# Product banks of PSUM in tiles of two, and rotary tables fetched one part earlier

## The chip, the cores and the metric

The kernel runs on one core of one Trainium2 chip, in one launch. The metric is the device time of one execution in microseconds (us). Three runs of the kernel before took 2540.79, 2544.62 and 2546.06 us; the median is 2544.62 us.

The engines are named as in the profile: PE (TensorE) multiplies matrices, PEld is its weight load, DVE is VectorE, ACT is ScalarE, POOL is GpSimd, and SP only issues transfers here. PE writes its products into PSUM, of which the program uses eight banks of 128 x 512 fp32. Another engine has to read a product out of its bank (evacuate it) before that bank can take a new one.

## The reference, cut to what matters

The first block is a hybrid mixer (projections, dilated window attention, a chunked state-space scan) and a feed-forward part. The second block has two layers on two streams of 256 positions, x and ctx, each 1024 wide:

```
for l in range(2):
    x  = x  + 0.5 * mx[2] * swiglu_2(modulate(rms_norm(x),  mx[0], mx[1]), *ffn1)
    xc = xc + 0.5 * mc[2] * swiglu_2(modulate(rms_norm(xc), mc[0], mc[1]), *ffn1)
    h, hc = modulate(rms_norm(x), ...), modulate(rms_norm(xc), ...)
    y, y_c = mix_window_diff(h, hc, ..., rope_head)          # layer 0
    y, _   = mix_mla_neighbourhood(h, hc, ..., rope_mla)     # layer 1
    x = x + mx[5] * y
    x = x + 0.5 * mx[8] * swiglu_2(modulate(rms_norm(x), mx[6], mx[7]), *ffn2)
    (layer 0 does the last two for xc, too)

def swiglu_2(h, w_gate, w_up, w_down):
    return (jax.nn.silu(h @ w_gate) * (h @ w_up)) @ w_down
```

`mx` and `mc` are nine vectors each, products of the condition with `w_mod`. `rope_head` and `rope_mla` are tables of cosines and sines that turn queries and keys. Layer 0 mixes by a windowed attention with sinks and a differential one (each head has two score maps); layer 1 by a latent attention (queries of six latent blocks, `cq`) and a neighbourhood attention with a bias looked up in `d_rpb`. All is fp32.

## The kernel before, in words

Every weight is loaded as fp32 and split in two: ACT casts it to a reduced form (`wh`, L114), DVE subtracts that from it (`wl`, L115). Activations are split likewise (`ah` and `al`, or `hh` and `hl`). A product of 128 output rows is a unit: for each of eight blocks of the contraction three matmuls, `wh*ah`, `wh*al`, `wl*ah` (L133 to L135), 24 in all, into one bank. With both streams side by side a matmul is 512 columns wide, with one stream 256.

A feed-forward part (`ffn`) runs a gate unit and an up unit for each of 22 blocks of the hidden width, and 24 down units between and after them. The gate's product is evacuated by ACT (silu, L409), the up product by DVE (`g<-g,pm`, L413), then ACT casts `hh` (L119) and DVE subtracts `hl` (L120). Down units are evacuated by DVE into the residual (L443).

The products stand in a pool `ps` of four tiles of one bank, tile name `pm` (L79, `psum`, L163). Two other pools of two banks each hold small sums (`pt`, `pa`). Weights go through five buffers for the raw load (`wraw`) and five for the two parts; short-lived tiles share ten buffers (`t1`).

Between the units stand background pieces (`weave`): each loads 512 KB of `w_mod` into a `wraw` buffer, and DVE multiplies it with the condition, once for each stream (`junk`, L981). There are 144 of them.

The order of the instructions on each engine is fixed when the program is built: a list scheduler with its own cost model and priorities puts them in order, and pools hand out buffers in that order. On the chip each engine works through its own list, and waits on semaphores for the others. Nothing is reordered there.

The mixers (`mix_ab` of layer 0, `mix_cd` of layer 1) load their tables `cos` and `sin` at their start by two transfers that ACT issues (L1181, L1182; L1397, L1398). DVE multiplies them with gains into tables for queries and keys (L1093, L1094). In layer 1 DVE's list has these ahead of the x stream's normalized input (`y`, L351, which ACT shifts to `ah`, L355). At the same place POOL issues a write of 1778 KB to DRAM, `rpb` (L1404), from which biases of the neighbourhood attention are read later. The attention parts take a bank for the scores of each head (L1257, L1317, L1580, L1602): DVE finds the row maximum (L1265, L1321, L1549) and ACT takes the exponential (L1100).

Of the kernel before, what the change touches and what calls it, by code (L numbers as in the profile page):

```python
# [16 lines left out]
T = 256  # L17
# [51 lines left out]
class Builder:  # L69
    def __init__(self, ctx, tc, A):  # L70
# [8 lines left out]
        self.ps = ctx.enter_context(tc.tile_pool(name="ps", bufs=4, space=PSUM))  # L79
# [82 lines left out]

    def psum(self):  # L163
        return self.ps.tile([128, 512], F32, name="pm")
# [996 lines left out]
def mix_ab(K, streams):  # L1161
# [86 lines left out]
    def attend_a(s, t, half):  # L1248
# [5 lines left out]
        def scores():  # L1254
            for b in range(2):
                for kv in range(2):
                    rows = slice(64 * kv, 64 * kv + 64)  # L1257
                    p = K.psum()
                    nc.tensor.matmul(p[:, :nk], qa[s][rows, 2 * half + b, t * 128:(t + 1) * 128], ka[rows, k0:k0 + nk],  # L1259
                                     start=True, stop=True)  # L1260
                    if s == "x":
                        o = p[:, (1 - t) * 128:(2 - t) * 128]
                        nc.vector.tensor_tensor(o, o, amask[:, t], op=ALU.add)
                    m = mneg[:, kv, b:b + 1]
                    nc.vector.tensor_reduce(out=m, in_=p[:, :nk], axis=AX.X, op=ALU.max, negate=True)  # L1265
                    h = 4 * kv + 2 * half + b
                    nc.vector.tensor_tensor(m, m, nsink[:, h:h + 1], op=ALU.min)
                    pr[kv][b] = softmax_tail(K, sp, p, nk, m, den[:, kv, b:b + 1])
# [40 lines left out]
    def attend_b(s, t, hd):  # L1309
# [81 lines left out]
def mix_cd(K, streams):  # L1391
# [4 lines left out]
    cos, sin = K.t1("cos"), K.t1("sin")  # L1396
    nc.scalar.dma_start(cos[r96], A["mla_cos"])  # L1397
# [492 lines left out]
```

## Time and profile before

| what | us |
|---|---|
| median of three runs | 2544.62 |
| the profiled execution | 2545.32 |
| its span in the trace | 2543.5 |
| PE busy | 2457.1 (97%) |
| DVE busy | 1642.2 (65%) |
| ACT busy | 1070.2 (42%) |

The span is the time from the first to the last instruction of the profiled execution. An engine's busy time is a sum over the whole span; how near an engine is to being the bound differs from stage to stage. The stages, by their start in the trace: mixer of block 1 from 0, its feed-forward part from 460, layer 0 with feed-forward 1 from 670, `mix_ab` from 1040, its output from 1300, feed-forward 2 from 1330; layer 1 with feed-forward 1 from 1700, `mix_cd` from 2060, attention from 2243, output and feed-forward 2 from 2350.

### The profile page before, as it was taken

The page shows a single profiled execution, that of the slowest core. Times are in us where ns is not written, and L with a number is a line of the kernel's source. Part 1 is how long each engine was busy: PE and PEld are TensorE (multiplying, and loading weights), DVE is VectorE, ACT ScalarE, POOL GpSimd, SP SyncE. Part 2 cuts the span into 40 slices and gives each one's busy share as a digit, 9 for nine tenths or more (in the row PEclk, how much of TensorE's full clock was granted, in tenths as well). Part 3 has the DMA queues.
Part 4 walks back from the last instruction along what each step waited for, and adds up shares of the span by engine and source line. Part 5 has one row for each costly group of instructions (what it writes and reads, how often), then busy time and mean ns, then how long its engine had stood idle before and what let it go on. Part 6 is the DMA issues. An engine that isn't in the chain of part 4 may idle for free.

```text
span 2543.5 us, 38370 instructions
## 1 busy us (share of the span) xinstructions
PE 2457.1 (97%) x15104; PEld 2122.3 (83%) x15104; DVE 1642.2 (65%) x3009; ACT 1070.2 (42%) x1934; POOL 15.4 (1%) x20
## 2 busy tenths in 40 slices
PE   6999999999999999999999999999999968999999
PEld 6999999999988888885598888888888857866999
DVE  4667777787867564767767666566545344667554
ACT  4657565535522222436743222243222234555443
POOL 0000000000000000000000000000000000000000
PEclk9999899999999999999999999999999988999999
DMA  8555455676455553431025545325555342232563
GB/s 227 148 156 161 144 163 182 210 246 203 162 166 167 164 168 99 130 98 51 1 75 178 170 150 170 128 91 178 171 166 164 103 96 74 98 95 82 172 185 125
DMA packets 117204, 363.66 MB, mean 143 GB/s; under 512 B 21050, under 2 KB 28730, under 8 KB 117024
## 3 DMA queue, kind: packets, MB, share of 16 engines
q1 hardware_dynamic: 114512, 355.73, 44.2%
q0 software_dynamic: 1008, 3.09, 1.0%
q10 hardware_dynamic: 1504, 2.40, 0.3%
q8 instruction: 119, 1.95, 0.3%
q14 instruction: 61, 0.50, 0.1%
HBM read 357.34 MB, written 3.82 MB: 142 GB/s over the span
## 4 chain that ended last, share of the span: by engine, by line
PE 70%; DVE 2%; DMA 2%; ACT 1%; issue 0%; ACTq 0%
PE pm L133 20%; PE pm L134 20%; PE pm L135 20%; PE pt L1120 1%; DMA sin<-mla_sin 1%; PE pa L1027 1%; PE pt L1051 1%; PE pa L1574 1%; PE pm L1319 1%; PE pm L1582 1%; PE pm L1259 0%; PE pa L1335 0%; PE pa L1296 0%; PE pm L1604 0%; PE pm L1145 0%; PE pa L1147 0%
## 5 line engine op out<-in xcount | busy, mean ns | idle before, releaser
L133 PE MATMUL pm<-ah,wh 128*128 128x256 f32 (+2 forms) x3096 | 1012.7, 329 | 46.4 <-ACT ah L355 35.6
L134 PE MATMUL pm<-al,wh 128*128 128x256 f32 (+2 forms) x3096 | 1007.1, 326 | 1.2 <-DVE al L356 1.1
L135 PE MATMUL pm<-ah,wl 128*128 128x256 f32 (+2 forms) x3096 | 1005.2, 325 | 0.0
L114 ACT CAST wh<-wraw 128x1024 fp32r<-128x1024 f32 (+4 forms) x535 | 540.3, 1013 | 1057.1 <-PE pm L134 850.0
L115 DVE TENSOR_TENSOR wl<-wraw,wh 128x1024 fp32r<-128x1024 f32 (+4 forms) x535 | 627.2, 1175 | 242.2 <-ACT wh L114 240.0
L133 PEld LDWEIGHTS pm<-ah,wh 128*128 128x128 f32 (+1 forms) x3096 | 588.6, 191 | 107.2 <-ACT ah L355 37.3
L134 PEld LDWEIGHTS pm<-al,wh 128*128 128x128 f32 (+1 forms) x3096 | 590.7, 191 | 54.2 <-issue 2.4
L135 PEld LDWEIGHTS pm<-ah,wl 128*128 128x128 f32 (+1 forms) x3096 | 590.6, 191 | 51.4 <-issue 1.7
L134 PE MATMUL pm<-hl,wh 128*128 128x512 f32 (+1 forms) x934 | 317.1, 339 | 0.0
L133 PE MATMUL pm<-hh,wh 128*128 128x512 f32 (+1 forms) x934 | 316.6, 339 | 0.0
L135 PE MATMUL pm<-hh,wl 128*128 128x512 f32 (+1 forms) x934 | 316.4, 339 | 0.0
L981 DVE SCALAR_TENSOR_TENSOR junk<-wraw,cactc 128x1024 f32<-128x1024 f32 x112 | 137.2, 1225 | 213.2 <-DMA wraw<-w_mod 212.8
L981 DVE SCALAR_TENSOR_TENSOR junk<-wraw,cactx 128x1024 f32<-128x1024 f32 x144 | 176.0, 1222 | 41.0 <-DMA wraw<-w_mod 38.6
L133 PEld LDWEIGHTS pm<-hh,wh 128*128 128x128 f32 x934 | 175.9, 188 | 21.2 <-issue 0.2
L135 PEld LDWEIGHTS pm<-hh,wl 128*128 128x128 f32 x934 | 175.9, 188 | 20.9
L134 PEld LDWEIGHTS pm<-hl,wh 128*128 128x128 f32 x934 | 175.9, 188 | 20.9
L119 ACT CAST hh<-g 128x512 fp32r<-128x512 f32 (+1 forms) x113 | 59.2, 526 | 162.1 <-DVE g L413 162.1
L413 DVE TENSOR_TENSOR g<-g,pm 128x512 f32<-128x512 f32 (+1 forms) x113 | 64.0, 566 | 58.7 <-PE pm L135 57.3
L120 DVE TENSOR_TENSOR hl<-g,hh 128x512 fp32r<-128x512 f32 (+1 forms) x113 | 63.8, 566 | 0.3
L409 ACT ACTIVATE g<-pm 128x512 f32<-128x512 f32 (+1 forms) x116 | 56.1, 489 | 2.5 <-PE pm L135 2.3
L443 DVE SCALAR_TENSOR_TENSOR xc<-pm,mcol0c,xc 128x256 f32<-128x256 f32 x56 | 26.9, 480 | 46.0 <-PE pm L135 45.8
L307 DVE TENSOR_TENSOR acc<-acc,sq 128x256 f32<-128x256 f32 x105 | 42.3, 419 | 13.7 <-ACT sq L306 13.4
(421 smaller groups left out, 2228.7 us busy)
## 6 DMA issues: line engine op xcount, KB each, us to landing
wraw<-w_mod SPq DMA_DIRECT2D x144, 512.0 KB, 4.1
wraw<-f1g SPq DMA_DIRECT2D x44, 512.0 KB, 3.7
wraw<-f1u SPq DMA_DIRECT2D x44, 512.0 KB, 4.2
wraw<-f2g SPq DMA_DIRECT2D x44, 512.0 KB, 3.7
wraw<-f2u SPq DMA_DIRECT2D x44, 512.0 KB, 4.0
wraw<-f1d SPq DMA_DIRECT2D x32, 512.0 KB, 4.0
wraw<-f2d SPq DMA_DIRECT2D x32, 512.0 KB, 3.7
wraw<-w_xbc SPq DMA_DIRECT2D x24, 512.0 KB, 3.6
```

What stands on the lines that cost most here:

```text
L114: nc.scalar.copy(h[:, :f], raw[:, :f])
L115: nc.vector.tensor_tensor(lo[:, :f], raw[:, :f], h[:, :f].bitcast(F32), op=ALU.subtract)
L119: self.nc.scalar.copy(h, src)
L120: self.nc.vector.tensor_tensor(lo, src, h.bitcast(F32), op=ALU.subtract)
L133: nc.tensor.matmul(out, h[:, c], ah, start=first, stop=False)
L134: nc.tensor.matmul(out, h[:, c], al, start=False, stop=False)
L135: nc.tensor.matmul(out, lo[:, c], ah, start=False, stop=last)
L307: nc.vector.tensor_tensor(self.acc[key], self.acc[key], sq, op=ALU.add)
L409: nc.scalar.activation(half(g["g"], s), p, AF.Silu)
L413: nc.vector.tensor_tensor(t, t, p, op=ALU.mult)
L443: self.nc.vector.scalar_tensor_tensor(x, p, gate, x, op0=ALU.mult, op1=ALU.add)
L981: nc.vector.scalar_tensor_tensor(junk, raw, 1.0, K.cact[s], op0=ALU.mult, op1=ALU.mult, accum_out=K.mcol[layer, s][:, j:j + 1])
```

## The change

The pool `ps` has two tiles of two banks instead of four of one. `psum()` hands out the first half of a tile, and at the next call its second half. `psum2()` hands out a whole tile, and the attention parts take one for the scores of two heads (or of two score maps); DVE then finds both row maxima in one instruction, adds masks and biases in one, and ACT takes two exponentials as before. The neighbourhood attention loads its biases for two heads at once. The tables `cos` and `sin` are fetched by a piece at the end of the preceding feed-forward part's list, by POOL's queue, into two of the ten `t1` buffers, where they stay until the mixer has used them.

```diff
@@ class Builder
-        self.ps = ctx.enter_context(tc.tile_pool(name="ps", bufs=4, space=PSUM))
+        self.ps = ctx.enter_context(tc.tile_pool(name="ps", bufs=2, space=PSUM))
+        self.half = None
...
+    def psum2(self):
+
+        self.half = None
+        return self.ps.tile([128, 2, 512], F32, name="pm")
+
     def psum(self):
-        return self.ps.tile([128, 512], F32, name="pm")
+
+        if self.half is None:
+            t = self.psum2()
+            self.half = t[:, 1]
+            return t[:, 0]
+        t, self.half = self.half, None
+        return t
@@ mix_ab (mix_cd likewise, with mla_cos, mla_sin)
-    cos, sin = K.t1("cos"), K.t1("sin")
-    nc.scalar.dma_start(cos, A["rope_cos"])
-    nc.scalar.dma_start(sin, A["rope_sin"])
+    cos, sin = K.rope
@@ differential attention
         def scores():
+            p = K.psum2()
             for m in range(2):
                 rows = slice(64 * m, 64 * m + 64)
-                p = K.psum()
-                nc.tensor.matmul(p[:, :nk], qb[s][rows, hd, t * 128:(t + 1) * 128], kb[rows, hd, k0:k0 + nk],
+                nc.tensor.matmul(p[:, m, :nk], qb[s][rows, hd, t * 128:(t + 1) * 128], kb[rows, hd, k0:k0 + nk],
                                  start=True, stop=True)
-                nc.vector.tensor_reduce(out=mneg[:, m:m + 1], in_=p[:, :nk], axis=AX.X, op=ALU.max, negate=True)
-                es.append(softmax_tail(K, sp, p, nk, mneg[:, m:m + 1], den[:, m:m + 1]))
+            nc.vector.tensor_reduce(out=mneg, in_=p[:, :, :nk], axis=AX.X, op=ALU.max, negate=True)
+            for m in range(2):
+                es.append(softmax_tail(K, sp, p[:, m], nk, mneg[:, m:m + 1], den[:, m:m + 1]))
...
@@ block2
+        def rope(layer=layer):
+
+            K.rope = K.t1("cos"), K.t1("sin")
+            rows = slice(0, 96 if layer else 128)
+            for t, n in zip(K.rope, ("cos", "sin")):
+                nc.gpsimd.dma_start(t[rows], A[("mla_" if layer else "rope_") + n])
+
         K.ffn(A[f"f1g{layer}"], A[f"f1u{layer}"], [A[f"f1d{layer}{i}"] for i in range(3)], both,
-              lambda s, m: K.mod(layer, s, 2)(m), hid_p, K.pieces(40), norms(3))
+              lambda s, m: K.mod(layer, s, 2)(m), hid_p, K.pieces(40) + [rope], norms(3))
```

The order of the instructions changes with it. Three places follow; the line numbers of the changed kernel are a little higher (L133 to L135 become L134 to L136, L413 becomes L425, L981 L993, L1093 L1105, L1441 L1450).

The first place is layer 0, feed-forward 2, at the end of an up unit of the 17th to 22nd hidden blocks. On PE, before, one unit follows another, each with a tile of its own (`pm_15885` is the up unit):

```order
L133 MATMUL pm_15885<-ah_5605,wh_15806 128x512
L134 MATMUL pm_15885<-al_5606,wh_15806 128x512
L135 MATMUL pm_15885<-ah_5605,wl_15807 128x512
L133 MATMUL pm_15927<-ah_5605,wh_15848 128x512
L134 MATMUL pm_15927<-al_5606,wh_15848 128x512
L135 MATMUL pm_15927<-ah_5605,wl_15849 128x512
```

Now the same up unit has the first half of `pm_15617` (weights `wh_15539`), the gate unit after it has the second half (`wh_15581`):

```order
L134 MATMUL pm_15617<-ah_5541,wh_15539 128x512
L135 MATMUL pm_15617<-al_5542,wh_15539 128x512
L136 MATMUL pm_15617<-ah_5541,wl_15540 128x512
L134 MATMUL pm_15697<-ah_5541,wh_15613 128x512
L135 MATMUL pm_15697<-al_5542,wh_15613 128x512
L136 MATMUL pm_15697<-ah_5541,wl_15614 128x512
L134 MATMUL pm_15697<-ah_5541,wh_15613 128x512
L134 MATMUL pm_15617<-ah_5541,wh_15581 128x512
L135 MATMUL pm_15617<-al_5542,wh_15581 128x512
```

Four matmuls of the next up unit (`pm_15697`, again the first half of its tile) have moved between the two. The first matmul of the second half waits on a semaphore for the DVE instruction that reads the first half (`g2_15609<-g2_15609,pm_15617`). So it is in 270 of the 333 tiles whose two halves are used by one: the second half's first matmul waits for the read of the first half.

On DVE at the same place, before, from the up product ahead of it to that of `pm_15885`:

```order
L413 TENSOR_TENSOR g2_15796<-g2_15796,pm_15810 128x512
L115 TENSOR_TENSOR wl_15924<-wraw_15921,wh_15923 128x1024
L120 TENSOR_TENSOR hl_15837<-g2_15796,hh_15836 128x512
L981 SCALAR_TENSOR_TENSOR junk_16075,mcol1x_5619<-wraw_16071,cactx_5613 128x1024
L115 TENSOR_TENSOR wl_15963<-wraw_15960,wh_15962 128x1024
L981 SCALAR_TENSOR_TENSOR junk_16112,mcol1c_5618<-wraw_16110,cactc_5610 128x1024
L981 SCALAR_TENSOR_TENSOR junk_16114,mcol1x_5619<-wraw_16110,cactx_5613 128x1024
L987 TENSOR_TENSOR mcol1c_5618<-mcol1c_5618,cols_83 128x8
L987 TENSOR_TENSOR mcol1x_5619<-mcol1x_5619,cols_83 128x8
L413 TENSOR_TENSOR g2_15877<-g2_15877,pm_15885 128x512
L115 TENSOR_TENSOR wl_16005<-wraw_16002,wh_16004 128x1024
```

And now, from `pm_15543` to `pm_15617`:

```order
L425 TENSOR_TENSOR g2_15529<-g2_15529,pm_15543 128x512
L116 TENSOR_TENSOR wl_15656<-wraw_15653,wh_15655 128x1024
L121 TENSOR_TENSOR hl_15570<-g2_15529,hh_15569 128x512
L993 SCALAR_TENSOR_TENSOR junk_15803,mcol1c_5554<-wraw_15801,cactc_5546 128x1024
L993 SCALAR_TENSOR_TENSOR junk_15805,mcol1x_5555<-wraw_15801,cactx_5549 128x1024
L116 TENSOR_TENSOR wl_15694<-wraw_15691,wh_15693 128x1024
L993 SCALAR_TENSOR_TENSOR junk_15841,mcol1c_5554<-wraw_15839,cactc_5546 128x1024
L993 SCALAR_TENSOR_TENSOR junk_15843,mcol1x_5555<-wraw_15839,cactx_5549 128x1024
L999 TENSOR_TENSOR mcol1c_5554<-mcol1c_5554,cols_83 128x8
L999 TENSOR_TENSOR mcol1x_5555<-mcol1x_5555,cols_83 128x8
L425 TENSOR_TENSOR g2_15609<-g2_15609,pm_15617 128x512
```

Before, three `junk` and two `wl` stand between the two reads; now four `junk` and two `wl` do. The last read stands behind `junk` of the same piece in both lists.

The second place is the start of `mix_cd` in layer 1, on DVE. Before, from the sums (`v`) of the x stream to the first of its inputs `y`:

```order
L314 TENSOR_SCALAR v_19315<-pt_19312 128x2
L1083 MEMSET zero_19252 128x256
L307 TENSOR_TENSOR acc_19310<-acc_19310,sq_19352 128x256
L316 RECIPROCAL rs_19316<-rs_19316 128x2
L1093 TENSOR_SCALAR xc_5593<-cos_19227,cols_83 96x256
L1094 TENSOR_SCALAR xc_5593<-sin_19228,cols_83 96x256
L1093 TENSOR_SCALAR xc_5593<-cos_19227,cols_83 96x256
L351 SCALAR_TENSOR_TENSOR y_19358<-xx_90,mcol1x_5619,pt_19355 128x256
```

And now:

```order
L326 TENSOR_SCALAR v_19001<-pt_18998 128x2
L116 TENSOR_TENSOR wl_19009<-wraw_19006,wh_19008 128x1024
L328 RECIPROCAL rs_19002<-rs_19002 128x2
L116 TENSOR_TENSOR wl_19142<-wraw_19139,wh_19141 128x1024
L1105 TENSOR_SCALAR xc_5529<-cos_18531,cols_83 96x256
L1106 TENSOR_SCALAR xc_5529<-sin_18532,cols_83 96x256
L363 SCALAR_TENSOR_TENSOR y_19043<-xx_90,mcol1x_5555,pt_19040 128x256
```

Two weights' `wl` have moved ahead of the tables, one table instruction behind the inputs.

The third place is ACT a little later, at the evacuation of the latent query products (`vc<-pm`). Before, each of them stands alone in a tile:

```order
L114 CAST wh_19556<-wraw_19554 128x1024
L1441 COPY vc_19239<-pm_19461 128x256
L315 ACTIVATE rs_19493<-v_19492 128x2
L114 CAST wh_19595<-wraw_19593 128x1024
L303 ACTIVATE acc_19487<-vc_19239 128x256
L119 CAST hk_19264<-y_19500 128x256
L119 CAST hk_19264<-y_19504 128x256
L114 CAST wh_19630<-wraw_19628 128x768
L1441 COPY vc_19239<-pm_19514 128x256
```

Now two share a tile (`pm_19145`):

```order
L115 CAST wh_19239<-wraw_19237 128x1024
L1450 COPY vc_18925<-pm_19145 128x256
L327 ACTIVATE rs_19177<-v_19176 128x2
L115 CAST wh_19278<-wraw_19276 128x1024
L315 ACTIVATE acc_19171<-vc_18925 128x256
L120 CAST hk_18950<-y_19184 128x256
L120 CAST hk_18950<-y_19188 128x256
L115 CAST wh_19312<-wraw_19310 128x768
L1450 COPY vc_18925<-pm_19145 128x256
```

The casts of the weights (`wh`, the one of 768 columns is that of the product `cd_kr`) stand ahead of the copies as before, and the copy of a first half (L1450, the first of the two) is now what the second half's matmuls wait for. SP loads the weights in the order of use (six `cd_cq`, `cd_kr`, four `cd_dk`), each when a `wraw` buffer is free. In the changed program the fifth `cd_cq` waits for the cast of the first selector (`sel<-wraw`, L1076 before), the sixth for that of the second, `cd_kr` for `wl_19009` and the first `cd_dk` for `wl_19142`.

## Rows read from the trace of the kernel before

**Rows 1.** The page: busy time, share of the span, instructions.
```profile
PE 2457.1 (97%) x15104; PEld 2122.3 (83%) x15104; DVE 1642.2 (65%) x3009; ACT 1070.2 (42%) x1934; POOL 15.4 (1%) x20
```
**Rows 2.** Waits, whole span: engine, line, waited for: us, times, longest.
```profile
DVE junk L981 <- DMA wraw<-w_mod: 251.3, 112, 4.8
...
ACT hh L119 <- DVE g L413: 162.1, 70, 7.0
DVE xc L443 <- PE pm L135: 94.0, 44, 3.8
```
**Rows 3.** Waits of hh, by stretches 460 to 670, 670 to 1040, 1330 to 1690, 1700 to 2060.
```profile
ACT hh L119 <- DVE g L413: 33.5, 16, 4.4
...
ACT hh L119 <- DVE g L413: 47.3, 20, 5.1
...
ACT hh L119 <- DVE g L413: 66.6, 20, 7.0
...
ACT hh L119 <- DVE g L413: 12.6, 12, 2.1
```
**Rows 4.** Timeline of ACT, 1596 to 1634: start, us, instruction, idle before and releaser.
```profile
1595.81 1.05 ACT L114 CAST wh<-wraw 128x1024 fp32r<-128x1024 f32 x1 [4.03 <-PE pm L134]
...
1618.12 1.05 ACT L114 CAST wh<-wraw 128x1024 fp32r<-128x1024 f32 x1 [2.43 <-PE pm L134]
```
**Rows 5.** Timeline of DVE, 1600 to 1634.
```profile
1599.90 0.68 DVE L413 TENSOR_TENSOR g<-g,pm 128x512 f32<-128x512 f32 x1
...
1611.75 1.23 DVE L981 SCALAR_TENSOR_TENSOR junk<-wraw,cactc 128x1024 f32<-128x1024 f32 x1 [4.49 <-DMA wraw<-w_mod]
...
1612.91 0.68 DVE L413 TENSOR_TENSOR g<-g,pm 128x512 f32<-128x512 f32 x1
...
1622.41 1.23 DVE L981 SCALAR_TENSOR_TENSOR junk<-wraw,cactc 128x1024 f32<-128x1024 f32 x1 [4.80 <-DMA wraw<-w_mod]
...
1625.03 0.68 DVE L413 TENSOR_TENSOR g<-g,pm 128x512 f32<-128x512 f32 x1
...
1629.58 0.69 DVE L413 TENSOR_TENSOR g<-g,pm 128x512 f32<-128x512 f32 x1 [0.99 <-PE pm L135]
```
**Rows 6.** Timeline of PE, around 2106.
```profile
2106.64 1.22 PE L133 MATMUL pm<-ah,wh 128*128 128x256 f32 x4 [25.19 <-ACT ah L355]
```
**Rows 7.** Timeline of DVE, 2060 to 2117.
```profile
2072.70 0.81 DVE L1076 CAST sel<-wraw 48x640 fp32r<-48x640 f32 x2
...
2097.09 0.35 DVE L1093 TENSOR_SCALAR xc<-cos,cols 96x256 f32<-96x256 f32 x1 [17.63 <-DMA cos<-mla_cos]
2105.04 0.35 DVE L1094 TENSOR_SCALAR xc<-sin,cols 96x256 f32<-96x256 f32 x1 [7.60 <-DMA sin<-mla_sin]
```
**Rows 8.** Timeline of ACT, 2070 to 2118.
```profile
2077.81 0.42 ACT L303 ACTIVATE acc<-vd 128x256 f32<-128x256 f32 x1 [4.11 <-issue]
```
**Rows 9.** DMA issues, 2060 to 2120: count, KB each, median us to landing.
```profile
rpb<-xc POOLq DMA_DIRECT2D x1, 1778.0 KB, 39.7
...
wraw<-cd_kr SPq DMA_DIRECT2D x1, 384.0 KB, 35.8
```
**Rows 10.** The tile cd_kr: its issue, ns min/median/max, first and last start.
```profile
L107 SPq DMA_DIRECT2D wraw<-cd_kr x1: 4246/4246/4246, 2073.6 to 2073.6; - x1
```
**Rows 11.** Stretches: us, busy PE, PEld, DVE, ACT, POOL; PEclk, DMA share, GB/s.
```profile
1048.00:1054.00 6.00, 5.98 (x28) 5.98 (x29) 5.06 (x16) 1.81 (x5) 0.00 (x0) 0.52 0.00 1
...
2073.00:2106.00 33.00, 2.86 (x16) 2.54 (x15) 4.22 (x13) 3.09 (x10) 0.00 (x0) 0.57 0.57 89
2106.00:2115.00 9.00, 8.36 (x50) 8.37 (x51) 6.36 (x19) 3.62 (x9) 0.00 (x0) 0.67 0.30 61
```
**Rows 12.** Timeline of PE, 1030 to 1056.
```profile
1046.69 0.80 PE L133 MATMUL pm<-ah,wh 128*128 128x256 f32 x3 [1.59 <-ACT ah L355]
```
**Rows 13.** Two stretches of attention: columns as in rows 11.
```profile
1170.00:1280.00 110.00, 103.98 (x574) 62.63 (x574) 82.98 (x242) 81.87 (x211) 0.00 (x0) 0.95 0.04 13
2243.00:2320.00 77.00, 75.88 (x426) 42.41 (x425) 57.26 (x126) 49.79 (x114) 10.27 (x8) 1.00 0.23 57
```

More of the change, by code (lines that the diff above doesn't have):

```diff
@@ L1255, in scores @@
             for b in range(2):
+                p = K.psum2()
                 for kv in range(2):
                     rows = slice(64 * kv, 64 * kv + 64)
-                    p = K.psum()
[L1259 to L1268, printed above, removed]
+                    nc.tensor.matmul(p[:, kv, :nk], qa[s][rows, 2 * half + b, t * 128:(t + 1) * 128],
+                                     ka[rows, k0:k0 + nk], start=True, stop=True)
+                if s == "x":
+                    o = p[:, :, (1 - t) * 128:(2 - t) * 128]
+                    nc.vector.tensor_tensor(o, o, amask[:, t].unsqueeze(1).to_broadcast([128, 2, 128]), op=ALU.add)
+                m = mneg[:, :, b]
+                nc.vector.tensor_reduce(out=m, in_=p[:, :, :nk], axis=AX.X, op=ALU.max, negate=True)
+                nc.vector.tensor_tensor(m, m, heads(nsink, half)[:, :, b], op=ALU.min)
+                for kv in range(2):
+                    pr[kv][b] = softmax_tail(K, sp, p[:, kv], nk, mneg[:, kv, b:b + 1], den[:, kv, b:b + 1])
             nc.vector.tensor_tensor(es, mneg, heads(sink, half), op=ALU.add)
@@ L1395, in mix_cd @@
     full, r96 = slice(0, 128), slice(0, 96)
-    cos, sin = K.t1("cos"), K.t1("sin")
-    nc.scalar.dma_start(cos[r96], A["mla_cos"])
-    nc.scalar.dma_start(sin[r96], A["mla_sin"])
+    cos, sin = K.rope
     sw_mask = [p ^ 8 for p in range(32)]
@@ L1545, in first @@
             for t in range(2):
[L1546 to L1552 removed]
+                p = K.psum2()
+                scores(b, t, p)
+                m = mneg[:, :, t]
+                nc.vector.tensor_reduce(out=m, in_=p, axis=AX.X, op=ALU.max, negate=True)
+                if scale != 1.0:
+                    nc.vector.tensor_scalar(m, m, scale, None, op0=ALU.mult)
+                for e in range(2):
+                    pr[e, t] = softmax_tail(K, sp, p[:, e], 512, mneg[:, e, t:t + 1], den[:, e, t:t + 1], scale)
             nc.vector.reciprocal(den, den)
@@ L1578, in attend, with scores_c @@
         return [first, second]
-    def scores_c(b, e, t):
-        p = K.psum()
-        nc.tensor.matmul(p, qc[:, 2 * b + e, t * 128:(t + 1) * 128], kc[:, 2 * b + e], start=True, stop=True)
-        return p
+    def scores_c(b, t, p):
+        for e in range(2):
+            nc.tensor.matmul(p[:, e], qc[:, 2 * b + e, t * 128:(t + 1) * 128], kc[:, 2 * b + e], start=True, stop=True)
     dmask = sp.tile([128, T], F32, name="dmask")
@@ L1587, in mix_cd, with load_bias, scores_d @@
     biases = {}
[L1589 to L1606 removed]
+    def load_bias(b):
+        bias = biases[b] = sp.tile([128, 2, 2, T], F32, name="bias", bufs=2)
+        for e in range(2):
+            for t in range(2):
+                for rr in range(2):
+                    r = 2 * t + rr
+                    src = bass.AP(tensor=rpb.tensor, offset=rpb.offset + ((2 * b + e) * 7 + 3 - r) * 127 + 63,
+                                  ap=[[56 * 127 - 1, 64], [127, 4], [1, 64]])
+                    nc.sync.dma_start(bias[64 * rr:64 * rr + 64, e, t].rearrange("p (r c) -> p r c", r=4), src)
+            nc.gpsimd.tensor_tensor(bias[:, e], bias[:, e], dmask.unsqueeze(1).to_broadcast([128, 2, T]), op=ALU.add)
+    def scores_d(b, t, p):
+        if t == 0 and 0 < b < 3:
+            load_bias(b + 1)
+        for e in range(2):
+            rows = slice(64 * e, 64 * e + 64)
+            nc.tensor.matmul(p[:, e], qd[rows, b, t * 128:(t + 1) * 128], kd[rows, b], start=True, stop=True)
+        nc.vector.tensor_tensor(p[:, :, :T], p[:, :, :T], biases[b][:, :, t], op=ALU.add)
     load_bias(0)
```

25 lines of the change are left out of this document (1 added, 24 removed).

## The prediction, on record before the run

> **What bounds the kernel now.** I read the page first: PE is busy for 97% of the span [rows 1], so time is won or lost where PE waits. Then the waits of the whole span [rows 2]: DVE waits 251.3 us for pieces of w_mod, and ACT's hh cast stands idle 162.1 us, 70 times, until DVE has read an up product. The reader is to see that nothing of this costs PE anything: with four single banks a product may lie unread while PE goes on. How long one lies is in the two timelines of one stretch [rows 4, 5]. ACT's casts wait for a weight buffer, that is for the end of a unit on PE: 1595.81 and 1618.12, four units apart, so a unit takes 22.31 / 4 = 5.58 us and a matmul 0.232. Up and gate units alternate, so up products end at 1595.8, 1607.0 and 1618.1. DVE has read them (start plus 0.68) at 1600.6, 1613.6 and 1625.7: 4.8, 6.6 and 7.6 us late, the last two just behind junk that waited 4.49 and 4.80 us for its load. The fourth, at 1629.58, waited for PE: on time. With four banks PE can be three units, 16.7 us, ahead of a read; 7.6 is far from that. Last I read the start of layer 1's mixer [rows 6 to 11], where PE stood still for 25.19 us.
>
> **The sum, part by part**, against the profiled execution's own 2545.32 us (span 2543.5 and 1.8 around it), 0.7 above the median.
>
> **Tables, layer 1.** PE's 25.19 us [rows 6] ended when DVE had waited 17.63 us for cos and 7.60 for sin [rows 7]; the write of rpb, 1778 KB, takes 39.7 us and everything issued beside it is late: cd_kr takes 35.8 [rows 9]. Loaded in the feed-forward part, the tables wait for nothing. The issue on ACT, which kept it for 4.11 us [rows 8], goes too, and about as much comes ahead of the inputs on DVE, two wl. So DVE, which had come to the tables at 2097.09 - 17.63 = 2079.5, is there at much the same time, and PE starts 1.6 us behind them as before (2106.64 - 2105.04), at some 2081 instead of 2106.6.
>
> What is late next are the weights behind the same write. The fifth cq weight is now loaded after the selector's cast (2072.70 [rows 7]), so beside rpb: it lands between cos (2097.1) and cd_kr (2073.6 + 35.8 = 2109.4 [rows 9, 10]), about 2098. Its cast stands on ACT ahead of the copy that the second half of the first query pair waits for. PE does two key units and one query unit (256 columns, half the width, so 5.58 / 2 = 2.8 us each) to 2089.5, stands until about 2099.5, does the next two to 2104.5, and stands again: the next copies are behind cd_kr's cast, cd_kr waits for a wl and lands about 2111, and cast and copies take 2 us more. From 2113 three units less five matmuls (7.8 us) bring PE to cd_kr's unit at 2121. Before, it came there at 2106.6 + 8 x 2.8 + 3.0 = 2132.0; the 3.0 is the clock, granted at 0.67 of 2.4 GHz, a mix of both levels, over 9 us behind the pause [rows 11]. That is 11 us; two pauses of 9 us will cost about 2 us of clock again, so I take **-9**. Ends: -28 if no weight is late (25.19 + 3.0), +1 if the pauses grow to all that was there and two of ten t1 buffers, held over the last down units, cost a little.
>
> **Tables, layer 0.** PE waited 1.59 us for the inputs [rows 12] and ran at a granted clock of 0.52, nearly all of it the lower level (1.2 of 2.4 GHz), over 6 us soon after (2.9 us lost) [rows 11]. The tables are only a part of what stands ahead of the inputs: **-2**, ends -4.5 and 0.
>
> **Scores.** In pairs DVE has 88 instructions fewer; two row maxima are joined, two additions of masks and biases. But PE is busy for 103.98 of 110 us and 75.88 of 77 in these stretches [rows 13]: DVE's saving lies beside it. On the other side two banks come free only together. **+0.5**, ends -1 and +4.
>
> *By the Trainium skill, "Perfetto Trace Analysis", section "Optimizing Scalar/DVE Operations", a DVE instruction that reads PSUM carries about 125 ns of overhead, and grouping improves throughput where the engine is saturated; 88 of them would be 11 us of DVE time, and if DVE were the bound the sum would come out 11 us lower. The rows above show another engine as the bound, so the sum does not take it.*
>
> **Halves.** The dependency is by tile: the first matmul of a second half waits until the first half has been read. Before, PE could be three units ahead of a read; now it is a few matmuls ahead (in the order shown four, 4 x 0.232 = 0.9 us). Where reads are prompt that is cover enough: DVE's reads of down products mostly waited for PE (94.0 us in 44 waits [rows 2]). The price is at the up products. hh's idle time measures their lateness, since it ends with DVE's read: 33.5, 47.3, 66.6 and 12.6 us in the four feed-forward parts [rows 3]. Whole, less the cover: 162.1 - 70 x 0.9 = 99 us. In layer 0's first part the gate is the first half; the price comes there all the same, as ACT's reads of gates stand behind the same hh. But a late read delays PE, and with PE later the next read is less late. In the stretch above, with the delay carried on, PE would lose 4.8 - 0.9 = 3.9, then 6.6 - 4.8 = 1.8, then 1.0: 6.7 us where the whole would be 3.9 + 5.7 + 6.7 = 16.3, a share of 0.41. 0.41 x 99 = 41, and 3 for the first pairs of block 1 and stray residual reads: **+44**. Low end: each part loses its longest single wait once, 4.4 + 5.1 + 7.0 + 2.1 = 19 [rows 3]. High end: the lateness forms anew each time, 99 + 5 = 104. I take the share of the one stretch that the rows show in full.
>
> Sum: 2545.3 - 9 - 2 + 0.5 + 44 = 2578.8; against the median 0.7 less, **2578 us**.
>
> **The rivals.** *The halves cost nothing.* The scheduler knows the dependency and could read first halves earlier; for it: the fourth read above was on time, and most gates are read within a unit. Against it: in the new order the up read still stands behind two pairs of junk, whose loads are what DVE waits for, and they come at the pace of buffers, not of the list. It gives 2544.6 - 10.5 = 2534.
>
> *The lateness stays tied to PE.* The junk's load waits for a buffer, the buffer for a wl, the wl for a cast, and the cast for the end of a PE unit [rows 4]. If that chain starts anew from PE's end, PE stands as long at every pair, and in pauses of that length the clock may fall as it did in layer 0. 2544.6 - 10.5 + 104 = 2638. It decides if reads stay 5 to 7 us late after PE has already been delayed. Against it: three reads in a row came 13.0 and 12.1 us apart where two units take 11.2, so DVE had a pace of its own there. *The Trainium skill, "Perfetto Trace Analysis", section "Matmuls", says that independent groups should rotate through different PSUM banks, so that reading one overlaps the next group's matmuls. The two halves are two banks, but the wait joins them; by that rule all of the lateness would show, which is this rival.*
>
> *Gain and loss cancel.* Tables at their full -28 - 4.5 and the halves at the low end, 2544.6 - 32.5 + 19 + 0.5 = 2532, or tables at -11 and halves at 11, near 2545. For it: no weight's lateness behind rpb cost anything so far. Against it: it needs two unlikely ends at once.
>
> **How the numbers follow.** Forecast, slower by the halves' waits: 0.70 (its own range 2555 to 2605). No cost of halves: 0.14, faster. Tied to PE: 0.08, slower. Cancelling: 0.08, of which 0.04 faster and 0.04 within. What a measurement of this kernel can tell from no change is about 0.2%, 5 us. So faster 0.18, same 0.05, slower 0.77. The range of 8 in 10 reaches from 2534, the first rival, to 2620, some way to the second.
>
> **What would show it.** In the changed trace PE idle behind DVE's read L425, some 60 times with 0.3 to 4 us, most in layer 0's second feed-forward part, and a wait of PE on ACT's L421 in its first; hh's idle time (L120) below 162. At the start of layer 1's mixer DVE's table instructions wait for nothing, PE starts near 2081 of the old time and stands twice until cd_kr has landed. If PE waits on L425 for less than 19 us in all, or PE's share of the span stays at 97%, the halves' term is wrong; if PE does not stand behind cd_kr's landing, the tables' term is.

## The result, and the profile after

The changed kernel takes 2682.9 us (median of 4 runs, 2672.68 to 2687.66) against 2542.7 us of before in the same session: a ratio of 1.0547, 95% interval 1.0511 to 1.0582. It is slower by 140 us where 33 were forecast; the direction was right, the size was not, and 2682.9 lies above the range of 2534 to 2620.

The page of the changed kernel, part 1, to be laid beside [rows 1]:

```profile
span 2680.8 us, 38234 instructions
...
PE 2538.5 (95%) x15104; PEld 2146.4 (80%) x15104; DVE 1644.6 (61%) x2921; ACT 1074.4 (40%) x1938; POOL 17.5 (1%) x24
```

The span is 137.3 us longer. PE has the same 15104 matmuls and is busy for 81.4 us more, idle for 55.9 us more. So a share of 95% hides more than half of the loss; why is shown below. DVE and ACT are busy for much the same time as before. The whole-span waits of the changed kernel that answer to [rows 2] (engine, line, waited for: us, times, longest):

```profile
DVE junk L993 <- DMA wraw<-w_mod: 218.6, 101, 4.7
...
DVE g L425 <- PE pm L136: 125.1, 57, 5.5
DVE xc L455 <- PE pm L136: 110.7, 57, 5.1
...
ACT hh L120 <- DVE g L425: 47.5, 39, 4.3
PEld pm L134 <- DVE g L425: 34.4, 63, 1.7
...
PEld pm L134 <- ACT g L421: 20.8, 48, 2.5
PEld pm L134 <- DVE xx L455: 20.8, 48, 2.7
...
PEld pm L134 <- ACT vc L1450: 16.9, 4, 10.7
...
PE pm L134 <- DVE g L425: 13.3, 24, 1.2
PE pm L134 <- DVE xx L455: 12.1, 12, 2.2
```

The direction of the waits has turned. Before, readers were late and PE did not care; now hh's idle time has fallen from 162.1 to 47.5 us, DVE waits for up products 57 times instead of 43, and PE's weight loads (PEld) wait for reads: 63 times for up products, 48 for gates, 48 for down products. L134 is the line of a unit's first matmul, in a first half as in a second; the trace's names do not tell the two apart, the program's order does.

The forecast's own sign misled: PE's row waits on L425 for 13.3 us in all, less than the 19 below which it called its halves' term wrong, while the loss is more than three times that term. The sign looked at up products alone, and PE's row does not show the waits of its weight loads.

Where the time went, stage by stage. The marks are the starts of DVE's last read of a stage's down products (L443 and its like), and of the first score matmul in the two attention parts; so every column is a difference of two starts in the trace (us):

```
                block 1          layer 0                     layer 1
                mixer    ff      ff 1   lin    attn   ff 2   ff 1   lin    attn   ff 2    span
before          457.6  201.8    379.6  105.8  172.6  376.0  378.7  170.6  100.4  200.2  2543.5
after           507.8  213.8    403.1  106.5  178.7  388.2  384.9  175.7  108.9  213.2  2680.8
e1_tables       451.1  202.8    380.8  100.9  171.0  377.4  379.6  158.0  100.4  200.1  2522.2
e2_banks        509.7  212.3    396.9  108.2  178.7  388.1  383.0  184.1  108.7  213.8  2683.7
e3_rotate       489.4  210.0    385.4  103.2  176.1  381.6  380.8  158.3  104.4  203.7  2592.9
e4_scoped       455.3  199.7    382.4  102.4  181.0  376.0  378.9  161.3  104.0  201.2  2542.3
e5_three        458.0  205.0    380.5  101.3  178.0  377.2  380.5  160.4  101.6  203.5  2546.0
e6_two          474.8  210.5    385.3  103.6  210.4  382.0  380.3  158.4  110.5  205.3  2621.0
e8_rpb          454.1  201.2    379.6  102.6  173.8  377.3  378.8  144.0  100.4  199.7  2511.5
e11_conv        500.6  211.8    400.0  108.9  179.9  388.3  384.0  176.0  108.5  213.7  2671.8
e10 (no w_mod)  452.7  199.1    379.9  100.8  173.7  377.6  379.9  152.7  100.4  200.1  2516.9
e9 (no w_mod)   508.7  208.4    386.0  106.5  178.6  381.9  382.7  175.9  108.5  214.3  2651.5
```

(ff is a feed-forward part, lin the products of a mixer up to its first score, attn the rest with the output.) Of the 137 us the mixer of block 1 has 50, the four feed-forward parts with background pieces 54, layer 1's last feed-forward part 13, the two other mixers 20. Of the four with pieces, layer 0's first lost most (23.5) and not its second (12.2), as the forecast had it.

### The profile page after: what moved, and what is told of

Read it like the earlier page. It is cut to its first block, busy times and chain, and to the rows that moved or that the text cites. A ratio compares the mean times of both kernels' runs of the same rounds, so it can differ in the third digit from the quotient of the medians.

```text
span 2680.8 us, 38234 instructions
## 1 busy us (share of the span) xinstructions
PE 2538.5 (95%) x15104; PEld 2146.4 (80%) x15104; DVE 1644.6 (61%) x2921; ACT 1074.4 (40%) x1938; POOL 17.5 (1%) x24
## 5 line engine op out<-in xcount | busy, mean ns | idle before, releaser
L134 PE MATMUL pm<-ah,wh 128*128 128x256 f32 (+2 forms) x3096 | 1031.0, 336 | 73.4 <-ACT vc L1450 15.8
L135 PE MATMUL pm<-al,wh 128*128 128x256 f32 (+2 forms) x3096 | 1017.8, 329 | 3.7 <-DVE al L368 2.6
L136 PE MATMUL pm<-ah,wl 128*128 128x256 f32 (+2 forms) x3096 | 1007.2, 328 | 0.0
L134 PEld LDWEIGHTS pm<-ah,wh 128*128 128x128 f32 (+1 forms) x3096 | 596.4, 193 | 167.8 <-DVE g L425 27.7
L135 PEld LDWEIGHTS pm<-al,wh 128*128 128x128 f32 (+1 forms) x3096 | 598.4, 193 | 57.2 <-DVE al L368 6.1
L136 PEld LDWEIGHTS pm<-ah,wl 128*128 128x128 f32 (+1 forms) x3096 | 595.6, 193 | 51.4 <-issue 1.3
L134 PE MATMUL pm<-hh,wh 128*128 128x512 f32 (+1 forms) x934 | 322.0, 346 | 11.2 <-DVE xx L455 7.6
L135 PE MATMUL pm<-hl,wh 128*128 128x512 f32 (+1 forms) x934 | 317.1, 340 | 0.0
L136 PE MATMUL pm<-hh,wl 128*128 128x512 f32 (+1 forms) x934 | 313.6, 340 | 0.0
L993 DVE SCALAR_TENSOR_TENSOR junk<-wraw,cactc 128x1024 f32<-128x1024 f32 x112 | 137.1, 1224 | 160.1 <-DMA wraw<-w_mod 160.0
L993 DVE SCALAR_TENSOR_TENSOR junk<-wraw,cactx 128x1024 f32<-128x1024 f32 x144 | 176.2, 1224 | 61.6 <-DMA wraw<-w_mod 58.6
L134 PEld LDWEIGHTS pm<-hh,wh 128*128 128x128 f32 x934 | 176.2, 189 | 45.5 <-DVE xx L455 16.5
L136 PEld LDWEIGHTS pm<-hh,wl 128*128 128x128 f32 x934 | 176.0, 189 | 21.2
L135 PEld LDWEIGHTS pm<-hl,wh 128*128 128x128 f32 x934 | 176.4, 189 | 19.9
L425 DVE TENSOR_TENSOR g<-g,pm 128x512 f32<-128x512 f32 (+1 forms) x113 | 64.1, 567 | 126.1 <-PE pm L136 125.1
L120 ACT CAST hh<-g 128x512 fp32r<-128x512 f32 (+1 forms) x113 | 59.3, 525 | 47.7 <-DVE g L425 47.5
L1132 PEld LDWEIGHTS pt<-ident,e 128*128 128x128 f32 x272 | 30.9, 146 | 28.3 <-issue 23.1
```

Of the source, the lines that this page charges most:

```text
L120: self.nc.scalar.copy(h, src)
L134: nc.tensor.matmul(out, h[:, c], ah, start=first, stop=False)
L135: nc.tensor.matmul(out, h[:, c], al, start=False, stop=False)
L136: nc.tensor.matmul(out, lo[:, c], ah, start=False, stop=last)
L425: nc.vector.tensor_tensor(t, t, p, op=ALU.mult)
L993: nc.vector.scalar_tensor_tensor(junk, raw, 1.0, K.cact[s], op0=ALU.mult, op1=ALU.mult, accum_out=K.mcol[layer, s][:, j:j + 1])
```

## The experiments

Two theories stood at the start. The halves theory: the loss is the wait of a second half for the read of the first, wherever a linear product is made. Against it, that the paired scores or the tables cost the time.

**e1_tables: the tables' part alone.**

```diff
-        self.ps = ctx.enter_context(tc.tile_pool(name="ps", bufs=2, space=PSUM))
+        self.ps = ctx.enter_context(tc.tile_pool(name="ps", bufs=4, space=PSUM))
...
 (scores by single heads, psum() as before; K.rope kept)
```

> The kernel before with the tables' part alone: fetched in the feed-forward part by POOL's queue; four single banks, scores by single heads. Halves theory (the 137 us of span come from second halves that wait for the read of first halves): 2533, 5 to 16 us faster than before, all of it at the two mixers' starts. Tables theory (the buffers held and the POOL queue cost the time): 2570 or more. With four banks PE should not stop behind the copies of the query products, so the gain in layer 1 may come to more than the 9 us forecast: up to 25.

Measured: 2526.45 us, ratio 0.993 (0.9905 to 0.9956). The tables are a gain of 18 us, a little more than the 5 to 16 expected. Layer 1's lin is 12.6 us shorter than before, layer 0's 4.9 (and its attn 1.6); block 1's mixer, where the tables change nothing of what is computed, differs by 6.5 in these two traces, at a granted clock of 0.97 before and 0.99 here. PE at the start of layer 1's mixer, e1_tables (start, us, instruction, idle before and releaser):

```profile
2070.18 1.22 PE L133 MATMUL pm<-ah,wh 128*128 128x256 f32 x4 [0.47 <-ACT ah L355]
...
2102.90 0.58 PE L133 MATMUL pm<-ah,wh 128*128 128x256 f32 x1 [9.27 <-ACT vc L1437]
```

The 25.19 us of [rows 6] are down to 0.47. What is late next is what the forecast named: the copies of the query products behind a weight's cast, here for 9.27 us. The expectation that PE would not stop there with four banks was wrong.

**e2_banks: tiles of two and paired scores, without the tables.**

```diff
-    cos, sin = K.rope
+    cos, sin = K.t1("cos"), K.t1("sin")
+    nc.scalar.dma_start(cos, A["rope_cos"])
+    nc.scalar.dma_start(sin, A["rope_sin"])
...
-              lambda s, m: K.mod(layer, s, 2)(m), hid_p, K.pieces(40) + [rope], norms(3))
+              lambda s, m: K.mod(layer, s, 2)(m), hid_p, K.pieces(40), norms(3))
```

> The changed kernel with the tables loaded where they were before: tiles of two banks and paired scores alone. Halves theory: 2690, what the tables gave lost again (2680 to 2700). Tables theory: under 2650.

Measured: 2684.73 us, ratio 1.0551 (1.053 to 1.0571). The banks are all of the loss, and beside them the tables are worth nothing that can be told: layer 1's lin is 8.4 us longer without them, layer 0's first feed-forward part 6.2 us shorter.

**e3_rotate: first halves of two tiles, then their second halves.**

```diff
-        if self.half is None:
-            t = self.psum2()
-            self.half = t[:, 1]
-            return t[:, 0]
-        t, self.half = self.half, None
-        return t
+        if not self.half:
+            t, u = self.psum2(), self.psum2()
+            self.half = [t[:, 0], u[:, 0], t[:, 1], u[:, 1]]
+        return self.half.pop(0)
```

> The changed kernel, but psum() takes two tiles and hands out first half, first half, second half, second half, so that a second half waits for a product that ended a whole unit earlier. Halves theory: the cover of a wait grows from 0.5 to 0.9 us to a unit (2.8 or 5.6 us), and nearly all comes back: 2550 to 2575. Rival, that what costs is the number of outstanding products or the release of two banks together: 2650 or more.

Measured: 2592.87 us, ratio 1.0191 (1.0171 to 1.021). Three lines of code that only change which half comes next give back 90 us; 18 more stay than the upper end expected. Of the 71 us that stay above e1_tables in these traces, 38 are in block 1's mixer. There a unit of cover is not enough.

**e4_scoped: tiles of two in the attention parts alone.**

```diff
+    def banks(self, pairs):
+
+        self.ps_ctx.close()
+        self.half, self.pairs = None, pairs
+        self.ps = self.ps_ctx.enter_context(self.tc.tile_pool(name="ps2" if pairs else "ps", bufs=2 if pairs else 4,
+                                                              space=PSUM))
...
+    K.banks(True)
     steps[0]()
...
     sx.close()
+    K.banks(False)
```

> The changed kernel with tiles of two banks only while the attention parts of layers 0 and 1 run; everywhere else four single banks as before. Halves theory: as e1_tables within 10 us, 2530 to 2545. Scores theory (paired scores free their banks late and cost the time): 2580 or more, and the added time stands in the attention parts.

Measured: 2546.88 us, ratio 1.0005 (0.9987 to 1.0023), a little above the expected range and 20 above e1_tables. Linear products are near their old times, so some 136 of the loss is theirs. But the two attention parts are 10.0 and 3.6 us longer than with single banks: the paired scores are a loss, not the +0.5 that was forecast. (The last linear unit of each mixer is inside too, and the change of pools belongs to this version alone; neither was tried by itself.) In layer 0's attention, e1_tables and then e4_scoped, columns as in [rows 11]:

```profile
1135.60:1306.70 171.10, 165.22 (x977) 116.67 (x978) 122.71 (x339) 107.31 (x264) 0.00 (x0) 0.97 0.12 38
...
1139.80:1320.80 181.00, 163.61 (x969) 116.26 (x969) 118.98 (x280) 109.66 (x262) 0.00 (x0) 0.93 0.11 36
```

PE is idle for 17.4 us instead of 5.9, and the granted clock is lower. The longest of these waits, e4_scoped:

```profile
PE pa L1355 <- ACT pts L1146: 3.7, 4, 1.5
PE pt L1141 <- DVE e L1346: 3.3, 2, 2.9
PE pt L1141 <- DVE e L1296: 3.2, 3, 2.1
```

PE waits there for exponentials (`e`) to be normalized or joined and for their transposes (`pts`) to be copied. Its waits for a bank for scores are 3.7 us against 3.3 in e1_tables.

**e5_three and e6_two: single banks, three and two instead of four** (otherwise e1_tables).

```diff
-        self.ps = ctx.enter_context(tc.tile_pool(name="ps", bufs=4, space=PSUM))
+        self.ps = ctx.enter_context(tc.tile_pool(name="ps", bufs=3, space=PSUM))
```

> The version with the tables' part alone (2526), with three single banks for products instead of four: PE may run two units ahead of a read. Theory that the distance counts which PE may run ahead of a read: within 10 us of 2526, since hardly a read before was two units late (up to 7.6 us, two units are 5.7 or 11.2), the loss in block 1 where units are short. Rival, that the 140 us came from something else in tiles of two (their joint release, the paired scores): no more than 3 us of loss.

> As e5_three, with two single banks: PE may run one unit ahead. Distance theory: as e3_rotate, where a second half also had one unit of cover, 2580 to 2595 with the loss stage by stage as there (block 1's mixer about 30). Rival: under 2550.

Measured: three banks 2552.06 us (1.0019, 1.0001 to 1.0037), two banks 2626.73 (1.0337, 1.0296 to 1.0378). Against e1_tables that is 26 and 100 us; by the ratios to the kernel before, as the sessions differ, 23 and 104. The loss falls with the distance that PE may run ahead of a read, so the distance theory holds in kind: in block 1's mixer 57 us with a few matmuls, 38 (e3_rotate) or 24 (e6_two) with one unit, 7 with two units, against three. In sizes the expectations missed: three banks cost 26 us, not under 10, of which 7 each in the mixer and in layer 0's attention; and two banks cost 39 us in that attention, which e3_rotate with its pairs had not shown. PE is idle there for 16.3 us against 5.9 in e1_tables, at a granted clock of 0.89 against 0.97.

**e9_after_nojunk and e10_tables_nojunk: without the background pieces** (the changed kernel, and e1_tables; w_mod is neither loaded nor multiplied).

```diff
-            raw = K.load_raw(K.A[f"w_mod{layer}"][j])
             for s in who:
-                junk = pool.tile([128, D], F32, name="junk")
-                nc.vector.scalar_tensor_tensor(junk, raw, 1.0, K.cact[s], op0=ALU.mult, op1=ALU.mult,
-                                               accum_out=K.mcol[layer, s][:, j:j + 1])
+                nc.vector.memset(K.mcol[layer, s][:, j:j + 1], 0.0)
```

> The changed kernel without the background pieces: w_mod is neither loaded nor multiplied, its columns are set to zero. Lateness theory (as forecast: PE stops because up products are read late behind junk): the feed-forward parts of layer 0 and the first of layer 1 lose nothing any more against e10_tables_nojunk, some 40 us less than with junk. Rival (a stop costs its time even when the read is prompt, since the last matmul, the read and the next weight load follow each other): each of them still loses 5 to 13 us, as layer 1's second part, which has no junk, lost 13.

> The version with the tables' part alone, also without the background pieces: the base for e9_after_nojunk. With four banks PE did not wait for reads behind junk, so its feed-forward parts take as long as with junk within 3 us each: 2510 to 2526.

Measured: 2653.4 us (1.043, 1.0413 to 1.0447) and 2522.82 (0.9915, 0.9896 to 0.9934). With four banks the pieces cost PE next to nothing (2526 against 2523), as expected; one feed-forward part, block 1's, is 3.7 us shorter without them, the others within 1. The four feed-forward parts that lose 11.0, 22.2, 10.8 and 5.3 us to the halves with junk (after less e1_tables) lose 9.3, 6.1, 4.3 and 2.8 without it. So of 49 us, 27 go with the pieces and 22 stay. That is between the two theories: two of the four parts reach the rival's 5 to 13, two do not. The waits of e9_after_nojunk's weight loads still number as many:

```profile
PEld pm L134 <- DVE g L425: 19.7, 56, 1.1
PEld pm L134 <- ACT g L421: 17.4, 47, 2.5
```

That all of the 22 is the price of prompt reads is not shown. A read is prompt where its engine waited for PE. DVE's reads of up products in layer 0's second part, 22 in all:

```profile
DVE g L425 <- PE pm L136: 56.9, 22, 3.1
```

All 22 waited, and so they do in layer 1's first part; there 4.3 and 2.8 us stay. In the two parts that lose more, prompt and late reads are not told apart.

**e11_conv: block 1's convolution products copied out at once.**

```diff
-            nc.scalar.activation(y, p, AF.Identity, scale=wcol(3), bias=cw[:, 96 + c:97 + c])
+            cp = K.t1("cp")
+            nc.scalar.copy(cp, p)
+            nc.scalar.activation(y, cp, AF.Identity, scale=wcol(3), bias=cw[:, 96 + c:97 + c])
             for j in (2, 1, 0):
                 sh = 3 - j
-                nc.vector.scalar_tensor_tensor(y[:, sh:], p[:, :T - sh], wcol(j), y[:, sh:], op0=ALU.mult, op1=ALU.add)
+                nc.vector.scalar_tensor_tensor(y[:, sh:], cp[:, :T - sh], wcol(j), y[:, sh:], op0=ALU.mult, op1=ALU.add)
```

> The changed kernel, but in block 1's mixer ACT copies each of the 24 convolution products out of its bank at once, and the convolution reads the copy; before, ACT and three DVE instructions read the bank one after the other. Theory that block 1's mixer lost its 50 us to late reads of such products: 10 to 25 us faster than the changed kernel (2658 to 2673), in block 1's mixer alone. Rival, that it lost them evenly at all of its products, by the plain time of a read and a new weight load: within 6 us of it, 2677 to 2689.

Measured: 2663.8 us (1.0448, 1.042 to 1.0476), 19 below the changed kernel, inside the expected range. Its profiled execution was the longest of its runs (2673.73), and shows 7.2 us less in block 1's mixer and 1.8 in all the parts behind it; the rest of the 19 stands in no trace. Late reads of these 24 products are a part of the mixer's 50 us, but where the gain is, the trace is nearer to the rival's 6 than to the expected 10 to 25. How the rest divides among its other products was not tried.

**e8_rpb: tables fetched early, and the bias rows copied within DRAM in layer 0's attention** (otherwise e1_tables).

```diff
-    rows = free[:8, 0:4].rearrange("p a t -> p (a t)")[:, :7 * 127]
-    nc.gpsimd.dma_start(rows, A["rpb"][:, 4:11].rearrange("h r c -> h (r c)"))
-    rpb = K.dram.tile([64, 8, 7 * 127], F32, name="rpb")
-    nc.gpsimd.dma_start(rpb.rearrange("q h u -> h q u"), rows.unsqueeze(1).to_broadcast([8, 64, 7 * 127]))
+    rpb = K.rpb
...
+    K.rpb = K.dram.tile([64, 8, 7 * 127], F32, name="rpb")
+    nc.gpsimd.dma_start(K.rpb[0:1, 0, 0:128], K.ACT["c"][0][0:1, 0, 0:128].bitcast(F32))
+    src = A["rpb"]
+    src = bass.AP(tensor=src.tensor, offset=src.offset + 4 * 127, ap=[[0, 64], [15 * 127, 8], [1, 7 * 127]])
+    nc.gpsimd.dma_start(K.rpb, src)
```

(The small transfer ahead of the large one only holds it back until layer 0's attention has its first output.)

> The version with the tables' part alone (2526), and the bias rows (rpb) copied within DRAM by one transfer in layer 0's attention, where the queues are nearly idle, instead of from SBUF at the start of layer 1's mixer. Theory that the weights of layer 1's mixer are late because of that write: PE's stop of 9.3 us behind the copies of query products goes, and some clock: 2512 to 2520. Rival, that these weights are late for want of buffers: 2526 or the write's time comes back in layer 0.

Measured: 2513.84 us (2507.27 to 2519.35), ratio 0.9865 (0.9843 to 0.9888): 34 us faster than before, and the fastest version here. Layer 1's lin is 13.9 us shorter than in e1_tables; layer 0's attn, where the copy now runs, is 2.8 longer. PE at its start, e8_rpb:

```profile
2073.30 1.22 PE L133 MATMUL pm<-ah,wh 128*128 128x256 f32 x4 [0.77 <-ACT ah L355]
```

and PE has no idle time in the rows of the 86 us behind it; `cd_kr`, 35.8 us to landing in [rows 9], takes 4.3:

```profile
DMA to landing us min/median/max: 4.3/4.3/4.3
```

So the lateness of those weights was the write's, not a want of buffers.

## Why the prediction was wrong in size

**The mechanism was the one named, but only a part of it was priced.** That tiles of two cost PE its freedom to run ahead of a read is what e2_banks, e3_rotate and e4_scoped show. By the Trainium skill, "Perfetto Trace Analysis", section "Matmuls", independent groups should rotate through banks so that a read overlaps the next group; e3_rotate, which rotates the same four banks in another order, gained 90 us by it.

**The step that failed** is "The price is at the up products. hh's idle time measures their lateness". It took all other reads as prompt ("Where reads are prompt that is cover enough"), at next to nothing. But a read can be late without any idle time, when its own engine has other work first. Layer 1's last feed-forward part has no junk and was priced at 0; it lost 13 us. PE there, in the changed kernel: the last matmul of a gate unit, which is a first half, and the first matmuls of the second half (from 2501.45). In the program's order eleven matmuls of the next gate unit stand between, the last two of them shown:

```profile
2499.82 0.28 PE L136 MATMUL pm<-ah,wl 128*128 128x256 f32 x1
...
2501.01 0.28 PE L134 MATMUL pm<-ah,wh 128*128 128x256 f32 x1
2501.13 0.28 PE L135 MATMUL pm<-al,wh 128*128 128x256 f32 x1
2501.45 0.39 PE L134 MATMUL pm<-ah,wh 128*128 128x256 f32 x1
2501.68 0.28 PE L135 MATMUL pm<-al,wh 128*128 128x256 f32 x1
```

the weight load ahead of it:

```profile
2501.45 0.19 PEld L134 LDWEIGHTS pm<-ah,wh 128*128 128x128 f32 x1 [0.25 <-ACT g L421]
...
2507.46 0.19 PEld L134 LDWEIGHTS pm<-ah,wh 128*128 128x128 f32 x1 [0.25 <-ACT g L421]
```

the read that it waits for, on ACT, and what ACT did before it:

```profile
2500.07 1.05 ACT L115 CAST wh<-wraw 128x1024 fp32r<-128x1024 f32 x1 [0.19 <-ACT hh L120]
2501.02 0.38 ACT L421 ACTIVATE g<-pm 128x256 f32<-128x256 f32 x1
...
2507.03 0.38 ACT L421 ACTIVATE g<-pm 128x256 f32<-128x256 f32 x1
```

and a prompt read for comparison, DVE's of the up product ahead, whose last matmul started at 2498.28:

```profile
2498.67 0.42 DVE L425 TENSOR_TENSOR g<-g,pm 128x256 f32<-128x256 f32 x1 [2.29 <-PE pm L136]
```

The prompt read starts 0.39 us behind the start of the last matmul. ACT could have read the gate so at 2499.82 + 0.39 = 2500.21 and been done by 2500.6 (an estimate), before PE came to the second half at 2501.25; it read at 2501.02, behind a weight's cast, 0.8 us late. So the cover would have been enough for a prompt read here, and the read was not prompt. At 20 of the part's 21 gates that are first halves ACT's read stands behind a weight's cast. Where up products are read promptly, tiles of two still cost 2.8 and 4.3 us a part (e9_after_nojunk), so that "cover enough" was nearly right; "prompt" was not.

Matmuls follow each other by 0.12 us; at the stop two gaps are 0.32 and 0.23. Two units take 2507.46 - 2501.45 = 6.01 us. Before, ACT's reads of gates in the same part, also two units apart:

```profile
2378.45 0.38 ACT L409 ACTIVATE g<-pm 128x256 f32<-128x256 f32 x1
2384.15 0.38 ACT L409 ACTIVATE g<-pm 128x256 f32<-128x256 f32 x1
```

5.70 us. So a stop costs 0.31 us, and if all 33 pairs of units cost as much, they make 10 of the part's 13 us. PE's row shows next to no idle time at the stop: a matmul counts 0.28 us as busy, more than the distance to the next, so a gap of 0.32 vanishes into it. Such stops are one source of PE's added busy time, a lower clock (below) the other, and they are why the share of PE was the wrong thing to watch. The waits of PEld show them.

**Block 1's mixer, priced at 3, cost 50.** The forecast measured lateness by hh's idle time alone [rows 3], which the mixer does not have. Its products are read by longer chains, in 2.8 us units. One tile in the changed kernel, with two convolution products: the last reader of its first half, and then the last three readers of its second half, on DVE, with another product's work between them:

```profile
193.74 0.47 DVE L676 SCALAR_TENSOR_TENSOR cv<-pm,cw,cv 128x253 f32<-128x253 f32 x1
...
200.33 0.48 DVE L676 SCALAR_TENSOR_TENSOR cv<-pm,cw,cv 128x255 f32<-128x255 f32 x1
200.72 0.42 DVE L587 TENSOR_TENSOR pa<-pa,bias 128x256 f32<-128x256 f32 x1
201.05 0.47 DVE L676 SCALAR_TENSOR_TENSOR cv<-pm,cw,cv 128x254 f32<-128x254 f32 x1
201.44 0.42 DVE L589 TENSOR_REDUCE mst<-pa 128x2 f32<-128x256 f32 x1
201.78 0.47 DVE L676 SCALAR_TENSOR_TENSOR cv<-pm,cw,cv 128x253 f32<-128x253 f32 x1
```

and PE, which starts a unit in a new tile when the last of them is done:

```profile
202.39 0.36 PE L134 MATMUL pm<-ah,wh 128*128 128x256 f32 x1 [3.09 <-DVE cv L676]
...
203.54 0.42 PE L134 MATMUL pm<-ah,wh 128*128 128x256 f32 x1
203.75 0.42 PE L135 MATMUL pm<-al,wh 128*128 128x256 f32 x1
203.97 0.42 PE L136 MATMUL pm<-ah,wl 128*128 128x256 f32 x1
```

In the program's order this unit is the first half of a tile (`pm_2152`) that takes the place of the one above (`pm_2021`). A tile comes free as a whole: its first half had been read at 194.21, 8 us before PE's start, but the tile's second half held it. That is a second wait, beside that of a second half for its first. The forecast has it for scores ("two banks come free only together") and puts it at nothing for linear products. In the mixer it is the larger one: of PE's stops of over 0.4 us behind reads, apart from one of 6.6 us that was there before as well, eight stand at the first half of a tile (11.9 us), four at a second half (6.0 us).

The rows show one more price. A microsecond behind the stop the matmuls follow each other by 0.21 instead of 0.12 us, for some 3 us: the lower of the clock's two levels (1.2 of 2.4 GHz). The mixer as a whole in the changed kernel, in e1_tables, and layer 0's second feed-forward part in the changed kernel, columns as in [rows 11]:

```profile
0.00:507.80 507.80, 459.02 (x3592) 424.70 (x3592) 323.67 (x577) 268.07 (x535) 3.78 (x10) 0.96 0.52 153
...
0.00:451.10 451.10, 431.73 (x3592) 408.92 (x3592) 322.18 (x578) 267.60 (x535) 3.78 (x10) 0.99 0.55 173
...
1409.90:1798.00 388.10, 379.78 (x1727) 305.16 (x1727) 242.80 (x388) 111.76 (x154) 0.00 (x0) 1.00 0.47 143
```

PE is idle for 48.8 us in the mixer instead of 19.4, and the granted clock is 0.96 instead of 0.99. Not every stop costs clock: in the feed-forward part, whose longest stop is 1.8 us, it stays at 1.00, and it does so after a stop of 2.97 us at 358.76 too. The mean granted clock is 0.980 before, 0.987 in e1_tables and 0.973 in the changed kernel; (1 - 0.973) x 2680.8 - (1 - 0.987) x 2522.2 = 72 - 33 = about 40 of the 158 us between these two traces. That is an estimate, as the mean counts time in which PE stands, too. The forecast's sum had a clock term for the tables and none for the halves.

**The other terms.** Late up products were priced at 41: the four feed-forward parts lost 49 against e1_tables, of which 27 go with the pieces (e9, e10) and 22 do not; so the share of 0.41, from one stretch, was on the high side, and that the sum came near was luck, by terms left out. Scores: 0.5 forecast, 10 and 4 (e4_scoped). "DVE's saving lies beside it" was right, but the exponentials come later in pairs, and PE waits for them; that one instruction for two row maxima, which waits for both scores, is what delays them is likely, and not shown. By the Trainium skill, "Perfetto Trace Analysis", section "Optimizing Scalar/DVE Operations", grouping can improve throughput if the engine is saturated; DVE was busy for 82.98 of 110 and 57.26 of 77 us in these stretches [rows 13], and here grouping cost time.

**Tables.** Layer 1's term was forecast with PE starting at once and standing twice. The changed kernel does so. DVE's table instructions wait for nothing:

```profile
2188.06 0.34 DVE L1105 TENSOR_SCALAR xc<-cos,cols 96x256 f32<-96x256 f32 x1
2188.33 0.34 DVE L1106 TENSOR_SCALAR xc<-sin,cols 96x256 f32<-96x256 f32 x1
```

and PE, against [rows 6]:

```profile
2189.65 0.50 PE L134 MATMUL pm<-ah,wh 128*128 128x256 f32 x2 [1.44 <-ACT ah L367]
2211.71 0.58 PE L134 MATMUL pm<-ah,wh 128*128 128x256 f32 x1 [10.54 <-ACT vc L1450]
...
2224.59 0.58 PE L134 MATMUL pm<-ah,wh 128*128 128x256 f32 x1 [4.54 <-ACT vc L1450]
```

The two stops are there, 10.54 and 4.54 us, at the copies named; ahead of the second, ACT had waited for `cd_kr`:

```profile
2223.43 0.83 ACT L115 CAST wh<-wraw 128x768 fp32r<-128x768 f32 x1 [0.66 <-DMA wraw<-cd_kr]
```

Against e2_banks, the same kernel without the tables' part, layer 1's lin is 8.4 us shorter, near the 9 forecast; with single banks it is 12.6, in layer 0 about 5 where 2 were forecast. Against the kernel before, layer 1's lin is 5.1 us longer all the same: the banks cost more there than the tables give.

Of the rivals, the one that tied lateness to PE came nearest in time (2638), but not by its reason, the chain of junk's loads: with junk gone, 131 us of difference stay.

## What to carry to other kernels

Before two products share a tile, ask how far the engine that writes may run ahead of the one that reads, in units of its own work: against three units, two cost 26 us here, one 66 to 100, the mixed distances of the changed kernel (a few matmuls for a second half, two units for a new tile) 156. Ask of every read what stands ahead of it on its reader's list: a read behind another job of 1 us is late though no engine shows idle time for it. Short stops of PE show in the waits of the weight loads, not in the busy share. And the order in which halves are handed out is as much a part of the design as their number.

## What was not expected of the hardware

- Stops of PE too short to show as idle time: two units at 256 columns took 6.01 us instead of 5.70, and PE's row has 0.04 us of idle time at the stop.
- A stop of 3.09 us was followed, about 1 us later, by some 3 us at the lower clock, one of 2.97 us was not; the mean over the run was 0.973, and 0.987 in e1_tables.
- The write of 1778 KB from 8 partitions took 39.7 us, and `cd_kr`, loaded beside it, 35.8 [rows 9]; the same bytes copied within DRAM, 64 rows first, landed in 11.0 us at a quiet time.
